# MLP block in four quarters: the up projection's product m2 by 512-column matmuls into four PSUM banks, in quarters 1 to 3

## Chip, cores and metric

One core of a Trainium2 chip runs the whole kernel in one launch. The metric is the device time of one execution in microseconds (us), the median of several runs. Engines are named as in the profile: PE is the TensorE matmul, PEld its weight load, DVE is VectorE, ACT is ScalarE, POOL is GpSimd, SP is SyncE.

## What is computed

The kernel is one decoder block: differential attention and causal pooling, merged by gates, and behind them an MLP. The change touches the MLP alone, the last half of the program. Cut to it, the reference reads:

```python
# SEQ = 512 rows, D_MODEL = 1024, D_FF = 4096, all float32
h2 = rmsnorm(x, norm_mlp_g[l])
z = jnp.square(jax.nn.relu(h2 @ w_up[l]))
x = x + (z @ w_down[l]).astype(x.dtype)
return rmsnorm(x, final_norm_g)
```

## The kernel before

**Quarters and products.** D_FF is cut into four quarters of 1024 columns. For quarter q the kernel runs `up(q)` and then `down(q)`, which adds the quarter's share of `z @ w_down` to `x1` in SBUF. Each of the two is a 2x2 block product done with seven block products in place of eight (a Strassen-type scheme). An operand block or a sum of blocks is called a form: A11, A12, A22 and S1 to S4. In quarters 1 to 3 the up projection's products are issued in this order: m1 (A11), m5 (S1), m6 (S2), m7 (S3), m4 (A22), m2 (A12, called the first block's second product), m3 (S4). m1, m6, m7 and m4 accumulate onto each other in the same banks, m5 and m3 in two others, m2 in its own.

**Precision.** Each float32 operand is cut into a high part that the PE takes (fp32r) and a low part that is the rest. A product is then high·high + high·low + low·high. For the weights ACT makes the high part (L112) and DVE the low part (L113). For z ACT makes the high part (L782) and DVE the low part (L785).

**Narrow and wide.** A product of the up projection has four units (i, p), of 128 d_ff rows each, with four weight blocks k. A narrow unit has 12 matmuls of 256 columns: for each k one of L821 (high weights by the high part of h2) and one of L824 (high weights by the low part), then four of L827 (low weights by the high part). Two units share one bank of 512 columns, so a narrow product takes two banks. A wide unit has 8: for each k one matmul of 512 columns (L818), whose moving operand is both parts of h2 side by side, then the four of L827 into the first half. Each wide unit fills a bank of its own, so the product takes four banks, and the two halves of a bank have yet to be added. In quarter 0 all products are narrow. In quarters 1 to 3 m1, m6, m7 and m4 are wide, and m5, m2 and m3 are narrow.

**Evictions.** `keep` copies a product out of PSUM into one of the float32 tiles `R` (rawz in the profile); for four banks it copies the second half with ACT (L850) and adds the first with DVE (L851). `join` adds a product to what lies in R already: by one add of 128x512 for each of two banks (L864), or, for four banks, by two adds of 128x256 for each bank (L860). `z_of` takes relu and square on ACT in halves of R (L873, L874). `sub` takes the differences of z blocks on DVE (L793, L796), and `zsplit` makes the two parts of a form of z. R[0] holds m1 + m2, and after `z_of` the form A11 of z (the tile z0); S1 of z is z4, A12 is z1, S2 is z5.

**Banks.** Two of the eight PSUM banks (2 and 3) are fixed, for the down projection's product m2 and what is summed on it; the other six are handed out in the order of a list, `acc.ids`. In names of the trace, um21_0 is the up projection's product m2, quarter 1, first bank; um11_0 to um11_3 are the four banks of m1, m6, m7 and m4; um51_0 and um51_1 those of m5 and m3; dm51 and dm11 are the down projection's first two products, S1 and A11, which take their banks from the same list.

**Down projection.** `down(q)` for q > 0 starts with S1, then A11, A12, S2, S4, S3, A22. `mms` issues, for each p, three matmuls: L932 (z high by weights high), L934 (z low by weights high), L935 (z high by weights low). `to_x1` adds finished banks to x1 on DVE (L952).

**What sets the order.** The program is written as a list of operations with their data. A scheduler turns it into one queue for each engine, and each engine works off its queue strictly in that order, waiting where a semaphore isn't there yet. An operation that is written down at one place can thus stand among operations of a later product. A few `after(...)` lines add an order by hand: among them, the weights' casts of quarter 3 for the up projection's A22 and S4 stand behind the joins that `state["joined", 0]` and `state["joined", 1]` name.

Of the kernel before, what the change touches and what calls it, by code (L numbers as in the profile page):

```python
# [51 lines left out]
def block_kernel(ctx, tc, xT, x_tok, gains, pos, consts, w_in, w_v, w_pool, w_out, w_up, w_dn, out):  # L52
# [4 lines left out]
    def after(later, earlier):  # L57
        tc.add_manual_dep(
            later.ins, earlier.ins.name,
            mybir.DependencyInfo(mybir.DependencyClass.NoSync, mybir.DependencyReason.DATA), reason="issue order",  # L60
        )

    state = {}
# [8 lines left out]
    def bank(i, name):  # L72
        return ps.tile([P, S], F32, tag=f"b{i}", name=name)
# [145 lines left out]
    for n in range(2):  # L219
        accs = [bank((0, 1, 2, 3, 4, 5, 6, 0)[4 * n + t], f"v{n}_{t}") for t in range(NT)]  # L220
        for kk in range(4):
# [24 lines left out]
            if n == 0 and 0 < kk < 3:  # L246
                i = kk - 1
# [94 lines left out]
    acc = Rot((0, 1, 2))  # L342
# [207 lines left out]
    A11, A12, A22, A21, S1, S2, S3, S4 = range(8)  # L550
# [18 lines left out]
    R = [rawz[:, i] for i in range(5)]  # L569
# [114 lines left out]
    acc = Rot((4, 5, 6, 7, 0, 1))  # L684
    m2 = [bank(2 + a, f"dm2_{a}") for a in range(2)]
# [84 lines left out]
    def halves(r):  # L770
        return [r[:, 2 * i : 2 * i + 2, :] for i in range(2)]
# [4 lines left out]
    def bank_view(pa):  # L776
        return [split_view(pa[i]) for i in range(2)]

    def zsplit(q, form, r):

        z = zform[form] = zf(f"z{form}_{q}")
        hi = zhi[q, form] = A.copy(out=z[:, 0], in_=r)  # L782
        if q == 0 and form == A11:
            after(hi, state[S4])
        lo = state["zlow", form] = V.tensor_tensor(out=z[:, 1], in0=r, in1=f(z[:, 0]), op=ALU.subtract)  # L785
        if q == 0 and form == A11:
            after(lo, state["join"])
# [10 lines left out]
    def up(q):  # L798
# [57 lines left out]
        def join(pa, r, hold=None):  # L856
            if len(pa) == 4:
                for i, ab in enumerate(map(split_view, pa)):
                    for j in range(2):
                        ins = V.tensor_tensor(out=r[:, i, :], in0=ab[:, j], in1=r[:, i, :], op=ALU.add)  # L860
                        state["joined", i] = ins
                return
            for a_, r_ in zip(bank_view(pa), halves(r)):
                state["join"] = V.tensor_tensor(out=r_, in0=a_, in1=r_, op=ALU.add)  # L864
                if hold:
                    after(state["join"], hold)

        def z_of(r, sign, pa=None):
            if pa and len(pa) == 4:
                keep(pa, r)  # L870
                pa = None
            for i, r_ in enumerate(halves(r)):
                A.activation(out=r_, in_=bank_view(pa)[i] if pa else r_, func=AF.Relu, scale=sign)  # L873
                ins = A.activation(out=r_, in_=r_, func=AF.Square)  # L874
            return ins

        wide = q > 0
        if wide:
            x, y, z = ((0, 1), (6, 7), (4, 5)) if q % 2 else ((4, 5), (6, 7), (0, 1))
            acc.ids, acc.n = x + y + z + x + y + x + z, 0  # L880
        ma = product(A11, "m1", wide=wide)
        keep(ma, R[0])
        if q == 0:
            forms_h2((S4,), slice(0, HS))

        def first_block():
            join(product(A12, "m2"), R[0], None if q else state[S2])
            z_of(R[0], 1.0)
            if q > 0:
                zsplit(q, A11, R[0])  # L890

        if q == 0:
            first_block()
# [3 lines left out]
        keep(ma, R[1])  # L897
        product(S3, "m7", onto=ma, wide=wide)
        join(ma, R[2])
        state["joined"] = state["join"]  # L900
        z_of(R[2], -1.0)
# [6 lines left out]
        if q > 0:  # L908
            first_block()
        product(S4, "m3", onto=mc)  # L910
        join(mc, R[1])
        z_of(R[1], -1.0)
        zsplit(q, A12, R[1])
# [118 lines left out]
    for q in range(4):  # L1032
        up(q)
        if q == 3:
            gfb, gmul = gain(big.tile([P, D], F32, tag="s4", name="gfb"), 1)
        down(q)
# [52 lines left out]
```

## Time and profile before

| | us |
|---|---|
| median of 3 runs | 669.75 |
| lowest and highest of them | 669.03, 670.06 |
| the profiled execution | 668.65 |
| its span, from first to last instruction | 666.8 |
| mean granted TensorE clock in it | 0.997 |

The times of single instructions all come from the profiled execution, whose own time is 668.65 us: 1.85 us more than its span, and 1.10 us less than the median. A row of a timeline reads: start in us from the span's start, duration in us, engine, line, operation, tile written <- tiles read, shape, how many follow each other (xcount), and in brackets the idle time before it with what ended it. A row of the windows gives the stretch, its length, and the busy us of each engine with the count of instructions in it.

In the timeline up(1) ends at 465.09 us, up(2) at 543.19 us and up(3) at 621.0 us, each with the last matmul of m3, and the first matmul of S1 in the down projection follows at once.

### The profile page before, as it was taken

How to read it: one execution, taken by the hardware profiler on the slowest of the kernel's cores; microseconds unless marked ns; L12 is line 12 of the kernel's file. 1: busy time of each engine (PE TensorE's matmuls, PEld its weight loads, DVE VectorE, ACT ScalarE, POOL GpSimd, SP SyncE). 2: the span in 40 equal slices, each digit the busy share in tenths (PEclk: the TensorE clock that was granted, in tenths of full speed). 3: DMA queues.
4: the chain of work that ended last, by engine and by line, in shares of the span. 5: the costliest groups of instructions: out<-in, count | busy, mean ns of one | idle time of the engine just before them, and what ended most of it. 6: DMA issues, size and time to landing. Idle time of an engine off the chain costs nothing.

```text
span 666.8 us, 9670 instructions
## 1 busy us (share of the span) xinstructions
PE 658.1 (99%) x3476; PEld 566.2 (85%) x3476; DVE 548.7 (82%) x958; ACT 470.3 (71%) x781; POOL 92.2 (14%) x115
## 2 busy tenths in 40 slices
PE   9999999999999999999999999999999999999995
PEld 7888888888888888888889988899889898899884
DVE  6855977799879987895688999777995889968996
ACT  8465587988878689976477975368563795456965
POOL 2001110031113011300202020202103021111020
PEclk9999999999999999999999999999999999999998
DMA  8416475355445466544886596786669676594863
GB/s 319 162 57 187 127 154 129 72 142 110 116 113 135 118 131 124 117 167 174 266 222 114 159 232 190 173 226 137 182 178 209 222 172 185 164 230 143 212 128 126
DMA packets 32736, 108.79 MB, mean 163 GB/s; under 512 B 4016, under 2 KB 4912, under 8 KB 32688
## 3 DMA queue, kind: packets, MB, share of 16 engines
q0 software_dynamic: 10512, 38.28, 32.1%
q1 hardware_dynamic: 21744, 69.38, 29.7%
q8 instruction: 27, 0.44, 0.3%
q10 hardware_dynamic: 432, 0.52, 0.2%
q14 instruction: 21, 0.17, 0.1%
HBM read 106.07 MB, written 2.10 MB: 162 GB/s over the span
## 4 chain that ended last, share of the span: by engine, by line
PE 98%; DMA 1%; ACT 0%; DVE 0%; SPq 0%; issue 0%
PE um L827 8%; PE dm L935 8%; PE dm L934 8%; PE dm L932 8%; PE um L818 7%; PE um L824 5%; PE um L821 5%; PE v L237 2%; PE o L430 2%; PE ga L137 2%; PE gp L133 2%; PE gp L137 2%; PE gp L134 2%; PE k L134 2%; PE ga L134 2%; PE k L133 2%
## 5 line engine op out<-in xcount | busy, mean ns | idle before, releaser
L934 PE MATMUL dm<-wh_dt,z 128*128 128x512 f32 (+1 forms) x128 | 49.4, 386 | 0.0
L935 PE MATMUL dm<-wl_dt,z 128*128 128x512 f32 (+1 forms) x128 | 49.0, 386 | 0.0
L112 ACT CAST wh_ut<-wga_uNone 128x1024 fp32r<-128x1024 f32 x24 | 25.1, 1054 | 33.7 <-DMA wga_uNone<-w_up 14.9
L932 PE MATMUL dm<-wh_dt,z 128*128 128x512 f32 (+1 forms) x128 | 48.6, 386 | 0.0
L952 DVE TENSOR_TENSOR x<-x,dm 128x512 f32<-128x512 f32 x48 | 32.4, 683 | 9.0 <-PE dm L935 8.8
L413 ACT ACTIVATE p<-p,st 128x128 f32<-128x128 f32 (+3 forms) x64 | 35.6, 557 | 5.8 <-DVE st L408 5.6
L782 ACT CAST z<-rawz 128x1024 fp32r<-128x1024 f32 x28 | 28.3, 1046 | 14.7 <-DVE rawz L793 13.0
L934 PE MATMUL dm<-wh_db,z 128*128 128x512 f32 x96 | 37.4, 391 | 0.0
L935 PE MATMUL dm<-wl_db,z 128*128 128x512 f32 x96 | 37.3, 390 | 0.0
L112 ACT CAST wh_ub<-wr_u 128x1024 fp32r<-128x1024 f32 x24 | 25.3, 1055 | 15.8 <-PE dm L934 5.3
L932 PE MATMUL dm<-wh_db,z 128*128 128x512 f32 x96 | 35.7, 389 | 0.0
L113 DVE TENSOR_TENSOR wl_ut<-wga_uNone,wh_ut 128x1024 fp32r<-128x1024 f32 x24 | 29.0, 1221 | 8.1 <-ACT wh_ut L112 8.0
L705 POOL DMA_DIRECT2D wga_dNone<-w_dn x16 | 13.8, 865 | 154.6 <-DVE wl_dt L113 154.4
L785 DVE TENSOR_TENSOR z<-rawz,z 128x1024 fp32r<-128x1024 f32 x28 | 33.3, 1219 | 1.5 <-ACT z L782 1.5
L112 ACT CAST wh_dt<-wga_dNone 128x1024 fp32r<-128x1024 f32 x24 | 24.8, 1045 | 11.5 <-DMA wga_dNone<-w_dn 6.4
L113 DVE TENSOR_TENSOR wl_ub<-wr_u,wh_ub 128x1024 fp32r<-128x1024 f32 x24 | 29.2, 1220 | 4.5 <-ACT wh_ub L112 4.5
L705 POOL DMA_DIRECT2D wga_uNone<-w_up x18 | 15.6, 864 | 111.2 <-DVE wl_ut L113 94.9
L827 PE MATMUL um<-gss,wl_ut 128*128 128x256 f32 x192 | 30.7, 282 | 0.0
L113 DVE TENSOR_TENSOR wl_dt<-wga_dNone,wh_dt 128x1024 fp32r<-128x1024 f32 x24 | 28.9, 1220 | 1.5 <-ACT wh_dt L112 1.5
L827 PEld LDWEIGHTS um<-gss,wl_ut 128*128 128x128 f32 x192 | 27.9, 190 | 2.0
L408 DVE CUSTOM_DVE_ANT_0 p<-s,mask 128x256 f32<-128x256 f32 (+3 forms) x52 | 27.2, 530 | 2.5 <-PE s L407 2.2
L934 PEld LDWEIGHTS dm<-wh_dt,z 128*128 128x128 f32 x128 | 24.0, 188 | 4.9
(335 smaller groups left out, 2191.6 us busy)
## 6 DMA issues: line engine op xcount, KB each, us to landing
wr_u<-w_up SPq DMA_DIRECT2D x24, 512.0 KB, 4.5
wr_d<-w_dn SPq DMA_DIRECT2D x24, 512.0 KB, 4.1
wga_uNone<-w_up POOLq DMA_DIRECT2D x18, 512.0 KB, 7.3
wga_dNone<-w_dn POOLq DMA_DIRECT2D x16, 512.0 KB, 6.8
wr_k<-w_in SPq DMA_DIRECT2D x8, 512.0 KB, 3.3
wr_ga<-w_in SPq DMA_DIRECT2D x8, 512.0 KB, 3.3
wr_gp<-w_in SPq DMA_DIRECT2D x8, 512.0 KB, 4.1
wl_ga<-w_in POOLq DMA_DIRECT2D x8, 512.0 KB, 6.3
```

The lines of the kernel that those rows point to most:

```text
L112: ins = A.copy(out=hi[:, sl], in_=raw[:, sl])
L113: state["low"] = (eng or G).tensor_tensor(out=lo[:, sl], in0=raw[:, sl], in1=f(hi)[:, sl], op=ALU.subtract)
L134: T.matmul(acc, lhsT=hi[:, c], rhs=rl[k], start=False, stop=False)
L413: A.activation(out=pr[:, c, :N], in_=pr[:, c, :N], func=AF.Exp, scale=-1.0, bias=st[:, c : c + 1], accum_out=st[:, 2 + c : 3 + c])
L785: lo = state["zlow", form] = V.tensor_tensor(out=z[:, 1], in0=r, in1=f(z[:, 0]), op=ALU.subtract)
L818: m = T.matmul(ab, lhsT=hi[:, c], rhs=both[:, k].rearrange("p a t -> p (a t)"), start=k == 0 and onto is None, stop=False, skip_group_chec ...
L821: m = T.matmul(a_, lhsT=hi[:, c], rhs=rh[:, k, :], start=p + k == 0 and onto is None, stop=False, skip_group_check=True)
L824: T.matmul(a_, lhsT=hi[:, c], rhs=rl[:, k, :], start=False, stop=False, skip_group_check=True)
L827: m = T.matmul(a_, lhsT=lo[:, c], rhs=rh[:, k, :], start=False, stop=k == 3, skip_group_check=True)
L932: m = T.matmul(a_, lhsT=zh, rhs=hi[:, sl], start=p == 0 and start, stop=False, skip_group_check=True)
L934: T.matmul(a_, lhsT=zl, rhs=hi[:, sl], start=False, stop=False, skip_group_check=True)
L935: end = T.matmul(a_, lhsT=zh, rhs=lo[:, sl], start=False, stop=p == 3, skip_group_check=True)
```

## The change

In quarters 1 to 3 m2 is wide as well. Its four banks need a place, so the three pairs of banks now rotate from quarter to quarter, and down's S1 takes m2's first pair and A11 its second. `join` of m2 takes the branch for four banks. Since `state["joined", i]` would now be overwritten by m2's join, it is set for R[2] alone (m7's join), as before.

```diff
                     for j in range(2):
                         ins = V.tensor_tensor(out=r[:, i, :], in0=ab[:, j], in1=r[:, i, :], op=ALU.add)
-                        state["joined", i] = ins
+                        if r is R[2]:
+                            state["joined", i] = ins
                 return
...
         wide = q > 0
         if wide:
-            x, y, z = ((0, 1), (6, 7), (4, 5)) if q % 2 else ((4, 5), (6, 7), (0, 1))
-            acc.ids, acc.n = x + y + z + x + y + x + z, 0
+            x, y, z = (((0, 1), (6, 7), (4, 5)), ((4, 5), (0, 1), (6, 7)), ((6, 7), (4, 5), (0, 1)))[q - 1]
+            acc.ids, acc.n = x + y + z + x + y + x + y + z, 0
         ma = product(A11, "m1", wide=wide)
...
         def first_block():
-            join(product(A12, "m2"), R[0], None if q else state[S2])
+            join(product(A12, "m2", wide=wide), R[0], None if q else state[S2])
             z_of(R[0], 1.0)
```

In counts: each of the three quarters has 32 matmuls of 512 and 256 columns for m2 (16 of L818, 16 of L827) where it had 48 of 256 columns, with as many weight loads; and 8 adds of 128x256 on DVE where it had 2 of 128x512. From line 861 on, lines of the changed kernel are numbered one higher: L864 is L865, L873 and L874 are L874 and L875, L932 to L935 are L933 to L936, L952 is L953.

The new instructions also stand at other places in the queues. First, PE at the end of up(1), where m2 is followed by m3's first bank (its second has been done by then) and that by down's S1. Before, all 24 matmuls of um21_0, all 24 of um21_1 and all 24 of um51_0 follow each other; the seam of the last two reads:

```order
L824 MATMUL um21_1_4408<-gab2_2979,wh_ub21_1_1_4403 128x256
L821 MATMUL um21_1_4408<-gab2_2979,wh_ub21_1_1_4403 128x256
L824 MATMUL um21_1_4408<-gab2_2979,wh_ub21_1_1_4403 128x256
L827 MATMUL um21_1_4408<-gab2_2979,wl_ub21_1_1_4404 128x256 x4
L821 MATMUL um51_0_4186<-gss3_2981,wh_ub22_1_0_4470 128x256
L824 MATMUL um51_0_4186<-gss3_2981,wh_ub22_1_0_4470 128x256
```

After, on the same engine at the same place:

```order
L827 MATMUL um21_1_4408<-gab2_2979,wl_ub21_1_0_4400 128x256 x4
L821 MATMUL um51_0_4186<-gss3_2981,wh_ub22_1_0_4462 128x256
L824 MATMUL um51_0_4186<-gss3_2981,wh_ub22_1_0_4462 128x256
L821 MATMUL um51_0_4186<-gss3_2981,wh_ub22_1_0_4462 128x256
L824 MATMUL um51_0_4186<-gss3_2981,wh_ub22_1_0_4462 128x256
L821 MATMUL um51_0_4186<-gss3_2981,wh_ub22_1_0_4462 128x256
L824 MATMUL um51_0_4186<-gss3_2981,wh_ub22_1_0_4462 128x256
L821 MATMUL um51_0_4186<-gss3_2981,wh_ub22_1_0_4462 128x256
L818 MATMUL um21_2_4409<-gab2_2979,wh_ub21_1_1_4403 128x512 x4
L827 MATMUL um21_2_4409<-gab2_2979,wl_ub21_1_1_4404 128x256 x4
```

m2's third bank now stands behind 7 matmuls of m3's first bank; its fourth stands 12 matmuls of m3 further on, and 5 of m3 follow it before down's S1.

Second, DVE at the same time, between the eviction of m4's third bank (um11_2) and that of m3's first bank (um51_0). Before:

```order
L851 TENSOR_TENSOR rawz_2982<-um11_2_4132,rawz_2982 128x256
L113 TENSOR_TENSOR wl_dt4_1_1_4567<-wga_dNone_1_1_4559,wh_dt4_1_1_4566 128x1024
L851 TENSOR_TENSOR rawz_2982<-um11_3_4133,rawz_2982 128x256
L864 TENSOR_TENSOR rawz_2982<-um21_0_4407,rawz_2982 128x512
L796 TENSOR_TENSOR rawz_2982<-rawz_2982 128x1024
L864 TENSOR_TENSOR rawz_2982<-um21_1_4408,rawz_2982 128x512
L785 TENSOR_TENSOR z4_1_4393<-rawz_2982,z4_1_4393 128x1024
L864 TENSOR_TENSOR rawz_2982<-um51_0_4186,rawz_2982 128x512
```

After:

```order
L851 TENSOR_TENSOR rawz_2982<-um11_2_4132,rawz_2982 128x256
L860 TENSOR_TENSOR rawz_2982<-um21_0_4407,rawz_2982 128x256
L113 TENSOR_TENSOR wl_dt4_1_1_4559<-wga_dNone_1_1_4551,wh_dt4_1_1_4558 128x1024
L860 TENSOR_TENSOR rawz_2982<-um21_0_4407,rawz_2982 128x256
L851 TENSOR_TENSOR rawz_2982<-um11_3_4133,rawz_2982 128x256
L860 TENSOR_TENSOR rawz_2982<-um21_1_4408,rawz_2982 128x256 x2
L860 TENSOR_TENSOR rawz_2982<-um21_2_4409,rawz_2982 128x256
L796 TENSOR_TENSOR rawz_2982<-rawz_2982 128x1024
L860 TENSOR_TENSOR rawz_2982<-um21_2_4409,rawz_2982 128x256
L860 TENSOR_TENSOR rawz_2982<-um21_3_4410,rawz_2982 128x256
L785 TENSOR_TENSOR z4_1_4393<-rawz_2982,z4_1_4393 128x1024
L860 TENSOR_TENSOR rawz_2982<-um21_3_4410,rawz_2982 128x256
```

One join now stands ahead of the weights' low part (L113), and the first join of the fourth bank stands ahead of the low part of z4 (L785). Behind these rows the queue of DVE is the same as before up to the low part of z1.

Third, ACT at the end of up(3) and the start of down(3), where z4, z0 and z1 are the forms S1, A11 and A12 of z, and wh_db11 and wh_db21 are weights of the down projection. Before:

```order
L782 CAST z4_3_5814<-rawz_2982 128x1024
L112 CAST wh_db11_3_0_6015<-wr_d0_3_0_5963 128x1024
L112 CAST wh_db11_3_1_6019<-wr_d0_3_1_5964 128x1024
L873 ACTIVATE rawz_2982<-rawz_2982 128x512
L874 ACTIVATE rawz_2982<-rawz_2982 128x512
L873 ACTIVATE rawz_2982<-rawz_2982 128x512
L782 CAST z0_3_5873<-rawz_2982 128x1024
L112 CAST wh_db21_3_0_6054<-wr21_d3_6051 128x1024
```

After:

```order
L782 CAST z4_3_5798<-rawz_2982 128x1024
L112 CAST wh_db11_3_0_5991<-wr_d0_3_0_5939 128x1024
L112 CAST wh_db11_3_1_5995<-wr_d0_3_1_5940 128x1024
L874 ACTIVATE rawz_2982<-rawz_2982 128x512 x2
L875 ACTIVATE rawz_2982<-rawz_2982 128x512 x2
L874 ACTIVATE rawz_2982<-rawz_2982 128x512
L782 CAST z0_3_5849<-rawz_2982 128x1024
L112 CAST wh_db21_3_0_6030<-wr21_d3_6027 128x1024
```

Ahead of the high part of z0 there are now three relus and two squares where there were two relus and one square. The last of these relus is that of the second half of m3's block, which needs DVE's join of um53_1.

On DVE, the queue of quarter 3 after z4's low part was: low part of wh_db11's first half, join of um53_0, low part of the second half, join of um53_1, z0's low part. The two joins of um23_3 now stand among these, and the x1 addition of dm53_0 stands ahead of z0's low part. In quarter 2 the low part of z1 now stands ahead of both low parts of wh_db21, and the low part of z5 behind both low parts of wh_dt5 (the weights of the down projection's S2), an x1 addition and an L793.

## Prediction

> **What bounds the kernel now.** I read the page first (share of busy time, then the chain that ended last), then the waits of PE, then the stretches around the change, then single rows.
>
> ```profile
> span 666.8 us, 9670 instructions
> PE 658.1 (99%) x3476; PEld 566.2 (85%) x3476; DVE 548.7 (82%) x958; ACT 470.3 (71%) x781; POOL 92.2 (14%) x115
> PE 98%; DMA 1%; ACT 0%; DVE 0%; SPq 0%; issue 0%
> ```
>
> PE is busy 99% of the span, and the chain runs on it for 98%. The view of PE's waits from 340 us to the end has no row. So any PE time that goes is gained, if PE finds its operands, and any new PE wait is lost. The average hides that DVE has room in one stage and none in the next:
>
> ```profile
> core 0: us, PE busy (x) PEld busy (x) DVE busy (x) ACT busy (x) POOL busy (x), PEclk, DMA share, GB/s
> 456.00:465.10 9.10, 9.10 (x78) 9.10 (x77) 6.45 (x8) 6.71 (x11) 3.51 (x4) 1.00 0.75 132
> 465.10:476.50 11.40, 11.40 (x53) 9.28 (x51) 11.19 (x12) 10.86 (x14) 0.00 (x0) 1.00 0.77 211
> 543.20:554.60 11.40, 11.40 (x53) 9.28 (x51) 11.22 (x13) 10.97 (x14) 0.00 (x0) 1.00 0.81 220
> 621.00:632.40 11.40, 11.40 (x53) 9.43 (x52) 11.40 (x13) 11.30 (x15) 0.00 (x0) 1.00 0.87 234
> ```
>
> The first row is the end of up(1), where m2 and half of m3 run; the other three are the first two products of down(1), down(2) and down(3). In these DVE is busy 11.19, 11.22 and 11.40 of 11.40 us. Work that slides over that border out of up(q) delays everything on DVE behind it, and PE reads its results there.
>
> **PE's saving.**
>
> ```profile
> 453.65 1.09 PE L818 MATMUL um<-gab,wh_ut 128*128 128x512 f32 x4
> 454.58 0.63 PE L827 MATMUL um<-gab,wl_ut 128*128 128x256 f32 x4
> 455.05 1.09 PE L818 MATMUL um<-gab,wh_ut 128*128 128x512 f32 x4
> 456.45 0.28 PE L821 MATMUL um<-gab,wh_ub 128*128 128x256 f32 x1
> 457.89 0.28 PE L821 MATMUL um<-gab,wh_ub 128*128 128x256 f32 x1
> ```
>
> A wide unit of m4 starts at 453.65 and the next at 455.05: 1.40 us. A narrow unit of m2 goes from 456.45 to 457.89: 1.44 us, twelve steps of 0.12. Four units a quarter give 4 x 0.04 = 0.16 us, and three quarters **0.48 us**. The PE ends m3 0.16 us earlier.
>
> The Trainium skill (TensorE: Matmul & The Clock Gate, Back-to-back issue gap) gives an isolated warm matmul N/2.4 + 2.5 ns, by which two of 256 columns in place of one of 512 cost 2.5 ns more: estimated from that page, 48 x 2.5 ns = 0.12 us, and the time would be 0.36 us above mine. The rows decide for 0.48.
>
> **DVE's price.**
>
> ```profile
> L860 DVE TENSOR_TENSOR rawz<-um,rawz 128x256 f32<-128x256 f32 x24 | 9.3, 417 | 0.1
> L864 DVE TENSOR_TENSOR rawz<-um,rawz 128x512 f32<-128x512 f32 x18 | 12.3, 686 | 1.6 <-PE um L827 1.6
> 450.17 0.75 DVE L860 TENSOR_TENSOR rawz<-um,rawz 128x256 f32<-128x256 f32 x2
> ```
>
> Eight adds of 417 ns replace two of 686: 1.96 us more busy time a quarter. Instructions overlap by some 0.085 us (two in a row take 0.75, so a step of 0.33; likewise 0.60 for 512 columns and 1.135 for 1024), so in steps the price is 8 x 0.33 - 2 x 0.60 = 1.45 us. The question is how much of it idle time takes in. Quarter 1 before:
>
> ```profile
> 457.77 1.23 DVE L113 TENSOR_TENSOR wl_dt<-wga_dNone,wh_dt 128x1024 fp32r<-128x1024 f32 x1 [0.63 <-ACT wh_dt L112]
> 458.91 0.42 DVE L851 TENSOR_TENSOR rawz<-um,rawz 128x256 f32<-128x256 f32 x1
> 459.53 0.69 DVE L864 TENSOR_TENSOR rawz<-um,rawz 128x512 f32<-128x512 f32 x1 [0.20 <-PE um L827]
> 461.44 1.23 DVE L796 TENSOR_TENSOR rawz<-rawz 128x1024 f32<-128x1024 f32 x1 [1.22 <-ACT rawz L874]
> 463.79 1.23 DVE L785 TENSOR_TENSOR z<-rawz,z 128x1024 fp32r<-128x1024 f32 x1 [0.52 <-ACT z L782]
> 465.29 0.69 DVE L864 TENSOR_TENSOR rawz<-um,rawz 128x512 f32<-128x512 f32 x1 [0.28 <-PE um L827]
> 475.15 2.35 DVE L785 TENSOR_TENSOR z<-rawz,z 128x1024 fp32r<-128x1024 f32 x2
> 465.09 0.63 PE L932 MATMUL dm<-wh_dt,z 128*128 128x512 f32 x2
> 465.56 0.39 PE L934 MATMUL dm<-wh_dt,z 128*128 128x512 f32 x1
> 476.45 0.47 PE L934 MATMUL dm<-wh_db,z 128*128 128x512 f32 x1
> ```
>
> The brackets add up to 0.63 + 0.20 + 1.22 + 0.52 + 0.28 = 2.85 us of idle time, twice the price; what counts is where it lies. Two lags: down's first matmul follows m3 at 465.09, and DVE starts m3's join at 465.29, 0.20 us behind PE. z1's low part ends at 475.15 + 1.22 = 476.37, and PE's L934, which takes 0.39 elsewhere, took 0.47 at 476.45, so its work began at about 476.53, 0.16 us behind DVE.
>
> **Quarter 1.** In the new order PE ends um21_0 at 456.45 + 1.40 = 457.85, um21_2 after 7 matmuls of m3 at 461.49, um21_3 after 12 more at 464.33, m3 at 464.93. On DVE the first join stands ahead of L113 and starts at 457.85 + 0.20 = 458.05; from there, in steps, L113 at 458.38, a join at 459.52, L851 at 459.85, two joins to 460.84. um21_2's join waits for PE to 461.69, and L796 follows at 462.02 (before: 461.44). um21_2's second join follows, then um21_3's first waits for PE till 464.53. Queued behind that wait is z4's low part: 464.86 to 466.09, where it ended at 465.02. PE wants it for L934 at 465.56 - 0.16 = 465.40 and gets it at 466.25: **0.85 us of new wait**. Behind it DVE runs um21_3's second join and reaches um51_0's at 466.33, where it was at 465.29. From there to z1's low part DVE was full before (11.19 of 11.40 us), so that part ends 1.0 us later. PE was already waiting for it a little (the 0.47), so all of the 1.0 comes through: 0.85 - 0.16 at z4, the rest at z1. Quarter 1: **+1.0**, between 0 (idle time takes all in) and 1.3 (all 1.45 comes through, less 0.16).
>
> **Quarter 2.**
>
> ```profile
> 543.39 0.69 DVE L864 TENSOR_TENSOR rawz<-um,rawz 128x512 f32<-128x512 f32 x1 [0.16 <-PE um L827]
> 546.97 1.22 DVE L785 TENSOR_TENSOR z<-rawz,z 128x1024 fp32r<-128x1024 f32 x1
> 554.55 0.47 PE L934 MATMUL dm<-wh_db,z 128*128 128x512 f32 x1
> 559.85 0.39 PE L934 MATMUL dm<-wh_dt,z 128*128 128x512 f32 x1
> ```
>
> L796 stands ahead of um22_2's and um22_3's joins, so z4's low part isn't late. Two joins (0.66) lie between it and z0's low part, of which idle time takes 0.16 to 0.25: z0 starts near 547.4. z1's low part is moved forward, so the short wait at 554.55 (0.08) goes. From z0's on, nine operations of 1024 columns (z0, z1, two of L793, one of L796, four of L113) and two additions now stand ahead of z5's low part: 547.4 + 9 x 1.135 + 2 x 0.60 = 558.8, and it ends at 560.0. PE wants it for L934 at 559.85, less 0.24, plus up to 0.45 as two matmuls of wh_db22 move ahead of it: 559.6 to 560.1, against 560.2 with the lag. A wait of 0.1 to 0.6, less 0.24: -0.1 to +0.4, and with the lateness of wh_db22's low parts up to +0.7. I take **+0.2**.
>
> **Quarter 3.**
>
> ```profile
> 622.83 0.69 DVE L864 TENSOR_TENSOR rawz<-um,rawz 128x512 f32<-128x512 f32 x1
> 623.43 1.22 DVE L785 TENSOR_TENSOR z<-rawz,z 128x1024 fp32r<-128x1024 f32 x1
> 630.31 2.35 DVE L785 TENSOR_TENSOR z<-rawz,z 128x1024 fp32r<-128x1024 f32 x2
> 622.36 1.04 ACT L782 CAST z<-rawz 128x1024 fp32r<-128x1024 f32 x1
> 626.95 0.39 PE L934 MATMUL dm<-wh_db,z 128*128 128x512 f32 x1
> 632.39 0.39 PE L934 MATMUL dm<-wh_db,z 128*128 128x512 f32 x1
> 645.85 0.50 PE L935 MATMUL dm<-wl_db,z 128*128 128x512 f32 x1
> ```
>
> um53_1's join ended at 622.83 + 0.69 = 623.52; two joins of um23_3 now stand before it: 624.2. On ACT z0's high part waited for no such join (622.36 to 623.40); now the relu that needs um53_1 stands ahead: it ends at about 624.8, the cast at 625.8, z0's low part at 627.1. PE wants that at 626.95 - 0.16 = 626.79 and gets it at 627.23: 0.44 us. Behind it DVE runs L793, an addition, two of L113 and L796 without a gap (625.85 + 5 x 1.135 + 0.60 = 632.1): z1's low part ends at 633.35, and PE, wanting it at 632.39 - 0.16 + 0.44 = 632.67, gets it at 633.51: 0.84. The row at 645.85 (0.50 in place of 0.39) shows that wl_db22, made by ACT behind z1's cast and then by a DMA, comes just in time: ACT's delay there may add 0 to 0.4, and I take 0.1. 0.44 + 0.84 + 0.10 - 0.16: **+1.2**.
>
> **Edits at nothing.** The rotation of banks: down's S1 takes um21_0's and um21_1's banks, whose last join ends at 460.9, and PE needs it at 464.9; A11 takes um21_2's and um21_3's, free at 466.4, needed 24 matmuls of 0.23 after 464.9, at 470.4. If that cover of 4 us went, PE would wait for the join. SP's queue is in the same order; on POOL one weight DMA of quarter 3 changes places with its neighbour, for which I count nothing, since PE has no wait there. `state["joined"]` names the same joins as before.
>
> **Sum.** 1.0 + 0.2 + 1.2 = +2.4 us, in which the 0.48 of PE is counted already: the profiled execution of 668.65 (span 666.8) would be 671.05, and the median, 1.10 above it, **672.15**. I forecast 672.2.
>
> **Rivals.**
> - **The joins are hidden (669.3).** In each quarter there is more idle time on DVE (2.85 us in quarter 1) than the joins cost (1.45), and only PE's 0.48 remains: 669.75 - 0.48. It decides at z4's low part: if it ends by 465.24, 0.16 ahead of PE's need at 465.40, nothing follows in quarter 1 but the full DVE; the ACT chain of quarter 3 would have to make up 0.4 as well. Against it stand 11.40 busy of 11.40 us. The Trainium skill (Perfetto Trace Analysis, Identifying the Most-Contended Engine) says that the engine with the highest occupancy is to be optimized first, here PE with its weight loads at 85% against DVE's 82%; by that the saving would count in full, and the stretches above, which it also tells one to look at apart, speak against it.
> - **Nothing is taken in (673.6).** All 1.45 come through in each quarter, as DVE reaches the border that much later and is full behind it: 3 x 1.45 - 0.48 = +3.9. It decides by whether um51_0's join in quarter 1 starts 1.0 or 1.45 us later; in quarter 2, z1's part ahead of its old place speaks against it.
> - **Weight loads bound (664).** In the first window PEld is busy 9.10 of 9.10 us, and 48 loads go; at a step of 0.12 each that is 5.8 us. Against it: the wide unit has 4 loads fewer and is only 0.04 us shorter.
> - That the change doesn't do what it says can be left out: the queues show the wide matmuls and the eight joins.
>
> **How the numbers follow.** About 0.2% (1.34 us) is what a measurement of this kernel tells from no change, so "same" is 668.41 to 671.09. Forecast 0.72, spread over the open ends of quarters 1 (0 to 1.0), 2 (-0.1 to 0.7) and 3 (0.7 to 1.6): 670.3 to 673.1. Hidden 0.16, nothing taken in 0.09, loads 0.03. The range 669.9 to 674.0 leaves out the hidden case and loads, most of 0.2. Same: 0.14 of the hidden case and 0.06 of the forecast's low end, 0.20; faster 0.05 (loads and 0.02 of the hidden case); slower 0.75.
>
> **What would show it.** Right: units of m2 at 1.40 us; DVE's L785 of z4 in quarter 1 behind a wait for um21_3, ending near 466.1; PE's waits on DVE's L785 at z4 and z1 of quarter 1 and z0 and z1 of quarter 3, some 0.4 to 0.9 us each, and nearly none in quarter 2. Wrong: no such waits (hidden), waits of like size in quarter 2 too (nothing taken in), a stretch of up(q) shorter by 1 us or more (loads).

## The result, and the profile after

| | before | changed |
|---|---|---|
| median of 6 runs, us | 669.90 | 674.35 |
| lowest and highest | 669.03, 670.33 | 672.63, 675.79 |
| profiled execution, us (span) | 668.65 (666.8) | 673.09 (671.3) |

The changed kernel is slower: 1.0067 of before, 95% interval 1.0056 to 1.0077. The forecast was 672.2, in a range of 669.9 to 674.0: the sign was right, the size was about half of what was measured (+2.4 against +4.45 us), and the measured time lies 0.35 us above the range.

The profiled execution of the changed kernel, its page and the view of PE's waits from 430 us on:

```profile
span 671.3 us, 9598 instructions
PE 660.4 (98%) x3428; PEld 563.5 (84%) x3428; DVE 552.5 (82%) x976; ACT 470.2 (70%) x781; POOL 92.0 (14%) x115
engine line waited for: us in total, times, longest us
PE dm L935 <- DVE z L785: 2.4, 5, 0.6
```

Before, that view of waits had no row. Now PE waits five times by this view, each time in a down projection, in front of the matmul that reads the low part of a form of z.

Where the time lies is read best by quarters. In the table a quarter runs from the first matmul of m5 in `up(q)` to that of the next quarter, and quarter 3 from there to PE's last matmul; the values are differences of starts in PE's timeline, in us.

| kernel | quarter 1 | quarter 2 | quarter 3 |
|---|---|---|---|
| before | 77.87 | 78.08 | 72.41 |
| changed | 78.81 | 79.56 | 74.38 |
| difference (forecast) | +0.94 (+1.0) | +1.48 (+0.2) | +1.97 (+1.2) |

Quarter 1 came as forecast; quarters 2 and 3 did not. Quarter 1, timeline of DVE and PE of the changed kernel:

```profile
456.53 1.09 PE L818 MATMUL um<-gab,wh_ub 128*128 128x512 f32 x4
457.94 1.09 PE L818 MATMUL um<-gab,wh_ub 128*128 128x512 f32 x4
458.13 0.42 DVE L860 TENSOR_TENSOR rawz<-um,rawz 128x256 f32<-128x256 f32 x1 [0.81 <-PE um L827]
461.78 0.42 DVE L860 TENSOR_TENSOR rawz<-um,rawz 128x256 f32<-128x256 f32 x1 [0.64 <-PE um L827]
464.61 0.42 DVE L860 TENSOR_TENSOR rawz<-um,rawz 128x256 f32<-128x256 f32 x1 [0.94 <-PE um L827]
464.95 1.22 DVE L785 TENSOR_TENSOR z<-rawz,z 128x1024 fp32r<-128x1024 f32 x1
466.42 0.68 DVE L865 TENSOR_TENSOR rawz<-um,rawz 128x512 f32<-128x512 f32 x1
466.23 0.50 PE L935 MATMUL dm<-wh_dt,z 128*128 128x512 f32 x1 [0.59 <-DVE z L785]
477.43 0.50 PE L935 MATMUL dm<-wh_db,z 128*128 128x512 f32 x1
```

A unit of m2 takes 1.41 us. DVE waits 0.94 us for m2's fourth bank with z4's low part queued behind, and that part ends at 466.17 (forecast 466.09). PE's L935 starts at 466.23 (forecast 466.25). Quarters 2 and 3, from the timelines of DVE, ACT and PE, first three rows of the kernel before and then the changed one:

```profile
533.23 1.22 DVE L743 TENSOR_TENSOR wga_dNone<-wr_d,wal_d 128x1024 f32<-128x1024 f32 x1
542.00 1.23 DVE L785 TENSOR_TENSOR z<-rawz,z 128x1024 fp32r<-128x1024 f32 x1 [0.52 <-ACT z L782]
610.96 1.22 DVE L743 TENSOR_TENSOR wga_dNone<-wr_d,wal_d 128x1024 f32<-128x1024 f32 x1 [1.69 <-DMA wr_d<-w_dn]
```

```profile
535.72 1.23 DVE L743 TENSOR_TENSOR wga_dNone<-wr_d,wal_d 128x1024 f32<-128x1024 f32 x1 [2.00 <-DMA wr_d<-w_dn]
543.91 1.23 DVE L785 TENSOR_TENSOR z<-rawz,z 128x1024 fp32r<-128x1024 f32 x1 [0.32 <-ACT z L782]
545.19 0.50 PE L935 MATMUL dm<-wh_dt,z 128*128 128x512 f32 x1 [0.46 <-DVE z L785]
547.57 0.63 ACT L874 ACTIVATE rawz<-rawz 128x512 f32<-128x512 f32 x1 [0.17 <-DVE rawz L860]
548.90 2.00 ACT L782 CAST z<-rawz 128x1024 fp32r<-128x1024 f32 x2
551.26 0.50 PE L935 MATMUL dm<-wh_db,z 128*128 128x512 f32 x1 [0.29 <-DVE z L785]
614.23 1.23 DVE L743 TENSOR_TENSOR wga_dNone<-wr_d,wal_d 128x1024 f32<-128x1024 f32 x1 [1.69 <-DMA wr_d<-w_dn]
626.77 0.68 DVE L865 TENSOR_TENSOR rawz<-um,rawz 128x512 f32<-128x512 f32 x1
627.53 0.62 ACT L874 ACTIVATE rawz<-rawz 128x512 f32<-128x512 f32 x1
628.05 1.03 ACT L782 CAST z<-rawz 128x1024 fp32r<-128x1024 f32 x1
629.12 1.23 DVE L785 TENSOR_TENSOR z<-rawz,z 128x1024 fp32r<-128x1024 f32 x1 [1.07 <-ACT z L782]
629.14 0.73 PE L933 MATMUL dm<-wh_db,z 128*128 128x512 f32 x2
630.40 0.50 PE L935 MATMUL dm<-wh_db,z 128*128 128x512 f32 x1 [0.53 <-DVE z L785]
636.67 0.50 PE L935 MATMUL dm<-wh_db,z 128*128 128x512 f32 x1 [0.54 <-DVE z L785]
```

In quarter 2 PE waits for z4 (545.19), which the prediction excluded, and for z0 (551.26), which it put at nothing. Behind the first stands a weight tile: DVE idles 2.00 us in front of L743, which needs down's last tile of first weights; before, it did not idle there. Behind the second stands ACT: a relu waits for DVE's last join of m2 (547.57), and z0's high part follows square after relu at 548.90. In quarter 3 DVE itself idles 1.07 us in front of z0's low part, waiting for ACT's cast; PE waits for the high part (629.14), for the low part (630.40), and for z1 (636.67). The weights of z4 are late here as well: L743 starts 24.75 us into quarter 3, and 23.98 us before.

### The profile page after: what moved, and what is told of

It is laid out like the page before. It is cut to its first block, busy times and chain, and to the rows that moved or that the text cites. A ratio compares the mean times of both kernels' runs of the same rounds, so it can differ in the third digit from the quotient of the medians.

```text
span 671.3 us, 9598 instructions
## 1 busy us (share of the span) xinstructions
PE 660.4 (98%) x3428; PEld 563.5 (84%) x3428; DVE 552.5 (82%) x976; ACT 470.2 (70%) x781; POOL 92.0 (14%) x115
## 4 chain that ended last, share of the span: by engine, by line
PE 51%; issue 26%; DMA 17%; DVE 4%; ACT 2%; POOL 0%; SPq 0%; POOLq 0%; ACTq 0%; DVEq 0%
DMA wga_uNone<-w_up 11%; DMA wga_dNone<-w_dn 5%; PE v L237 2%; PE o L430 2%; PE ga L137 2%; PE gp L133 2%; PE gp L134 2%; PE gp L137 2%; PE k L134 2%; PE ga L134 2%; PE k L133 2%; PE k L137 2%; PE ga L133 2%; PE v L239 2%; PE v L238 2%
## 5 line engine op out<-in xcount | busy, mean ns | idle before, releaser
L935 PE MATMUL dm<-wh_dt,z 128*128 128x512 f32 (+1 forms) x128 | 49.8, 389 | 1.1 <-DVE z L785 1.1
L936 PE MATMUL dm<-wl_dt,z 128*128 128x512 f32 (+1 forms) x128 | 49.0, 386 | 0.0
L933 PE MATMUL dm<-wh_dt,z 128*128 128x512 f32 (+1 forms) x128 | 48.8, 387 | 0.0
L953 DVE TENSOR_TENSOR x<-x,dm 128x512 f32<-128x512 f32 x48 | 32.0, 679 | 9.5 <-PE dm L936 9.3
L935 PE MATMUL dm<-wh_db,z 128*128 128x512 f32 x96 | 37.5, 394 | 1.4 <-DVE z L785 1.4
L936 PE MATMUL dm<-wl_db,z 128*128 128x512 f32 x96 | 37.1, 390 | 0.0
L113 DVE TENSOR_TENSOR wl_ut<-wga_uNone,wh_ut 128x1024 fp32r<-128x1024 f32 x24 | 29.0, 1220 | 9.7 <-ACT wh_ut L112 9.5
L785 DVE TENSOR_TENSOR z<-rawz,z 128x1024 fp32r<-128x1024 f32 x28 | 33.5, 1218 | 3.0 <-ACT z L782 3.0
L933 PE MATMUL dm<-wh_db,z 128*128 128x512 f32 x96 | 35.9, 391 | 0.1
L113 DVE TENSOR_TENSOR wl_ub<-wr_u,wh_ub 128x1024 fp32r<-128x1024 f32 x24 | 29.1, 1218 | 4.8 <-ACT wh_ub L112 4.7
L112 ACT CAST wh_dt<-wga_dNone 128x1024 fp32r<-128x1024 f32 x24 | 24.5, 1046 | 9.0 <-DMA wga_dNone<-w_dn 3.2
L827 PE MATMUL um<-gss,wl_ut 128*128 128x256 f32 x192 | 30.7, 282 | 0.0
L935 PEld LDWEIGHTS dm<-wh_dt,z 128*128 128x128 f32 x128 | 24.0, 188 | 7.0 <-DVE z L785 2.4
L827 PEld LDWEIGHTS um<-gss,wl_ut 128*128 128x128 f32 x192 | 27.9, 190 | 2.0
L113 DVE TENSOR_TENSOR wl_dt<-wga_dNone,wh_dt 128x1024 fp32r<-128x1024 f32 x24 | 28.6, 1216 | 0.7 <-ACT wh_dt L112 0.7
```

The costliest lines, as they stand in the source:

```text
L112: ins = A.copy(out=hi[:, sl], in_=raw[:, sl])
L113: state["low"] = (eng or G).tensor_tensor(out=lo[:, sl], in0=raw[:, sl], in1=f(hi)[:, sl], op=ALU.subtract)
L827: m = T.matmul(a_, lhsT=lo[:, c], rhs=rh[:, k, :], start=False, stop=k == 3, skip_group_check=True)
L933: m = T.matmul(a_, lhsT=zh, rhs=hi[:, sl], start=p == 0 and start, stop=False, skip_group_check=True)
L935: T.matmul(a_, lhsT=zl, rhs=hi[:, sl], start=False, stop=False, skip_group_check=True)
L936: end = T.matmul(a_, lhsT=zh, rhs=lo[:, sl], start=False, stop=p == 3, skip_group_check=True)
```

## Experiments

Two theories stood first. **Carried**: quarters 2 and 3 were sized right but come in late from the quarter before. **Local**: each pays its own price. Then, for the mechanism, **amount** (DVE does eight instructions for two) against **order** (m2's banks are finished late, and their joins fall among the low parts). Ratios are to runs of the kernel before on the same chip.

**m2 wide in one quarter alone** (`only_q1`, `only_q2`, `only_q3`).

```diff
-            join(product(A12, "m2", wide=wide), R[0], None if q else state[S2])
+            join(product(A12, "m2", wide=q == 1), R[0], None if q else state[S2])
```

(2 or 3 in place of 1; the banks rotate only in that quarter.)

> m2 is wide in quarter 1 alone. In the profile of the changed kernel quarter 1 cost PE +0.98 us net, quarter 2 +1.45, quarter 3 +1.95, against +1.0, +0.2 and +1.2 in the prediction. Theory 'carried': quarter 1 was sized right, and quarters 2 and 3 cost more than worked out because DVE and the weight loads come into them already late from the quarter before. It expects +1.0 us here at the end of quarter 1, of which quarters 2 and 3 keep all: about 670.9 (before 669.9). Theory 'local': each quarter pays only its own price, wherever the others stand: also 670.9. If the loss is made good later (slack behind quarter 1), 669.9.

> m2 is wide in quarter 2 alone. 'Carried': without quarter 1's lateness the price is that of the prediction, +0.2 (up to +0.7): 670.1 to 670.6. 'Local': +1.45 as in the changed kernel's profile: 671.3.

> m2 is wide in quarter 3 alone. 'Carried': the prediction's price of +1.2: 671.1, with the last join of m3 (um53_1) ending about 0.7 us after its place before. 'Local': +1.95: 671.9, with that join about 1.4 us later than before.

Measured, in this order: 671.51 (1.0026, 1.0016 to 1.0036), 671.16 (1.0018, 1.0006 to 1.0029) and 671.62 us (1.0034, 1.0023 to 1.0045), with before at 669.52. The quarter concerned took 78.77, 79.67 and 74.26 us. Quarters 2 and 3 cost as much alone as they do together, and the three ratios add up to 1.0078, not below the 1.0067 of the whole change, so "carried" falls as it was worded: the prices do not shrink to those of the prediction. That they are local is not shown. `only_q1` costs 1.7 us (1.0026), more than the +1.0 of both theories, and its quarter 2, which is the kernel before's, took 78.73 us; in four profiles whose first two quarters are both the kernel before's it took 78.08 to 78.43. So a little of quarter 1's change seems to reach quarter 2. And the waits are not the same ones. With quarter 2 alone z4 comes in time, and PE waits in up(2), in front of m4, instead; the like times of 79.67 and 79.56 us are made of different waits. With quarter 3 alone the weights of z4 come in time (L743 starts 23.74 us into the quarter), PE hardly waits for z0 (a step of 0.31 us in front of the row at 627.88, where 0.23 is the rule), and its longest wait is for wl_db22. Here are the row of quarter 2 alone and three of quarter 3 alone:

```profile
527.03 1.20 PE L818 MATMUL um<-gab,wh_ut 128*128 128x512 f32 x4 [0.47 <-DVE rawz L860]
```

```profile
611.72 1.22 DVE L743 TENSOR_TENSOR wga_dNone<-wr_d,wal_d 128x1024 f32<-128x1024 f32 x1 [1.47 <-DMA wr_d<-w_dn]
627.88 0.50 PE L938 MATMUL dm<-wh_db,z 128*128 128x512 f32 x1
648.46 0.50 PE L939 MATMUL dm<-wl_db,z 128*128 128x512 f32 x1 [0.64 <-DMA wl_db<-w_dn]
```

ACT prepares the tile wl_db22 and a DMA completes it: ACT's last step of it (L722) ended 15.81 us behind the first matmul of down(3), 14.66 before, and the tile landed at 26.5 us, 24.8 before. In the changed kernel it landed at 26.6 us; PE does not wait for it there because it has already lost 2.0 us in front of z0 and z1. In profiles whose quarter 3 is unchanged this wait was also 0 to 0.6 us, so part of it comes and goes.

**m3's first bank behind m2** (`m2_first`).

```diff
             elif form == S4:
                 after(first[-1], state["m4"])
+                if q:
+                    after(first[-1], state["m2"])
+            elif form == A12 and q:
+                state["m2"] = m
```

> As the changed kernel in all three quarters, but m3's first bank may not start on PE before m2's last matmul, so that the four banks of m2 are finished one behind the other and joined while PE runs m3. Same instructions, other order. Theory 'order' (the price comes from the late third and fourth bank of m2, whose joins fall among the low parts of z and of the weights): in quarter 1 the fourth bank is done on PE near 462.1 instead of 464.3 and z4's low part ends near 465.4, so that only PE's saving is left: about 669.5 to 670.0. Theory 'amount' (DVE has eight adds in place of two and no room for the 1.45 us a quarter, wherever they stand): 673 to 674.4.

Measured: 670.50 us, 1.0013 (1.0003 to 1.0024). The same instructions in another order cost 0.9 us in place of 4.5. Quarter 1 took 78.13 us, quarter 2 79.03, quarter 3 72.28. DVE and PE in quarter 1:

```profile
461.41 1.09 DVE L864 TENSOR_TENSOR rawz<-um,rawz 128x256 f32<-128x256 f32 x3 [0.25 <-PE um L827]
463.54 0.88 DVE L864 TENSOR_TENSOR rawz<-um,rawz 128x256 f32<-128x256 f32 x2
464.75 1.23 DVE L785 TENSOR_TENSOR z<-rawz,z 128x1024 fp32r<-128x1024 f32 x1 [0.33 <-ACT z L782]
466.03 0.50 PE L939 MATMUL dm<-wh_dt,z 128*128 128x512 f32 x1
```

All joins are done by 464.42, 1.07 us before PE starts down's S1 at 465.49 in this profile, and z4's low part waits for ACT alone. That is for "order", but not all of it: quarter 2 keeps 0.95 us, and the time lies 0.5 us above the top of what "order" expected.

**Half of the joins left out (`half_join`); eight DVE instructions on narrow banks (`eight`).** The first keeps the order and takes the amount away, the second does the reverse. The result of `half_join` lacks the left-out product, and that of `eight` is another because of the maxima.

```diff
-                    for j in range(2):
+                    for j in range(2 if r is R[2] else 1):
```

```diff
+                if q and r is R[0]:
+                    for j in range(2):
+                        state["join"] = V.tensor_tensor(out=r_[:, j], in0=a_[:, j], in1=r_[:, j], op=ALU.add)
+                        V.tensor_tensor(out=r_[:, j], in0=r_[:, j], in1=a_[:, j], op=ALU.max)
+                    continue
```

> As the changed kernel, but m2's second half of each bank (its product with the low part of h2) is left out of the join: four adds of 128x256 a quarter in place of eight, 1.32 us of steps where the kernel before has 1.20. PE is as in the changed kernel. Theory 'amount' (DVE's extra time is the price, wherever it stands): nearly no extra time is left, 669.5 to 669.9. Theory 'order' (the price comes from joins that wait for m2's late fourth bank, in front of z's low part): that join still stands ahead of z4's low part and waits until 464.5, so each quarter keeps about 0.7 us: 671 to 672, with a PE wait of 0.7 to 0.9 us in front of L935 at the start of the down projection in quarter 1.

> The kernel before (m2 narrow, in two banks), but DVE does eight instructions of 128x256 for m2's join in each quarter: four adds, and four maxima of the result with the same bank that are no part of the computation. DVE's load is that of the changed kernel without its late banks. 'Amount': 3 x 1.45 us come through as in the changed kernel, and PE saves nothing: 674 to 675. 'Order': m2's banks are done before m3, so the eight fall into DVE's idle time: 669.9 to 671.

Half the joins: 671.20 us, 1.0029 (1.0018 to 1.0040), quarters at 78.46, 79.43 and 73.42. PE at the start of down(1):

```profile
466.08 0.50 PE L935 MATMUL dm<-wh_dt,z 128*128 128x512 f32 x1 [0.47 <-DVE z L785]
```

The step from the matmul before (465.22) is 0.86 us where 0.23 is the rule: with DVE's load almost that of before, the wait behind m2's late bank stays. Eight on narrow banks: 670.31 us, 1.0016 (1.0006 to 1.0026), and the same matmul follows without a wait:

```profile
465.89 0.39 PE L939 MATMUL dm<-wh_dt,z 128*128 128x512 f32 x1
```

Its quarters 1 and 2 took 77.85 and 78.14 us, as before: the eight instructions themselves are hidden there. Quarter 3 took 73.73, with one long wait for wl_db22 (a step of 1.20 us). Both speak for "order", and against "amount" as the whole cause. Behind the late banks the amount does count: with four joins there in place of eight the price is 1.9 us and not 4.5.

**The late joins behind z4, the last relu behind z0** (`places`).

```diff
+                        elif i == 3:
+                            after(ins, state["zlow", S1])
...
+                if q and i and r is R[1]:
+                    after(ins, zhi[q, A11])
```

> The changed kernel with two orders added: the joins of m2's fourth bank stand behind z4's low part on DVE (this moves them in quarter 1; they were there in quarters 2 and 3), and the last relu of m3's block behind z0's high part on ACT (quarter 3). Theory 'full DVE' (what is moved away from z4 comes back at z1, since DVE works without a gap from there to z1's low part): quarter 1 stays within 0.2 us of the changed kernel's 78.8 us (from down's first weights of m5 in one quarter to those in the next, 77.9 before), with the wait at z4 nearly gone and that at z1 longer by as much; in all 673.5 to 674.3. Theory 'each wait by itself': the wait of 0.75 at z4 goes and nothing takes its place, 78.1 us, and 673.0 or less in all.

Measured: 673.15 us, 1.0059 (1.0046 to 1.0072); quarters at 78.50, 79.14 and 73.21. The start of down(1) and of its A12:

```profile
466.49 0.39 PE L939 MATMUL dm<-wh_dt,z 128*128 128x512 f32 x1
478.40 0.50 PE L939 MATMUL dm<-wh_db,z 128*128 128x512 f32 x1 [0.57 <-DVE z L785]
```

The wait for z4 is gone, and the step in front of z1's low part has grown from 0.42 us to 1.02. Of 0.76 us taken away at z4 0.6 came back at z1: in quarter 1 "full DVE" is nearly right (78.50, 0.3 below the changed kernel, where 0.2 was allowed). In quarter 3 PE no longer waits for z0, and the quarter takes 1.17 us less. But this does not show that the relu was the cause: the weights of z4 came earlier in this profile as well (L743 starts 23.66 us into the quarter, in the changed kernel 24.75), and with quarter 3 alone, where the relu does stand in z0's way, PE hardly waited for z0 either. (The work behind PE's last matmul took 8.40 us in this profile and 7.46 in the others, so not all of this reaches the time.)

**The rotation of banks alone** (`rotate`).

```diff
+            acc.ids, acc.n = x + y + z + x + x + y + z, 0
```

> The kernel before with the new rotation of banks alone: m2 is narrow in the first pair, down's S1 takes that same pair, A11 the second, and the pairs rotate. If the banks cost nothing, as predicted: 669.9 within 0.3. If the rotation makes a first matmul wait for a join, 670.5 or more, with a PE wait in front of down's S1 or A11, or of the next quarter's m1.

Measured: 669.56 against 669.27 us, 1.0011 (1.0001 to 1.0020), with quarters 1 and 2 at 77.85 and 77.91 and no wait of PE in front of S1, A11 or m1. So no bank makes PE wait. Quarter 3 took 73.00 us, 0.6 more than before, with a PE wait for wl_db22; whether the rotation has a part in that is not shown.

**Two profiles more.**

> The kernel before once more, for a second profile. In kernels whose quarter 2 is the kernel before's, the second weight tile of down(2) landed 25.3 us (m2 wide in quarter 1 alone) after down's first weights of m5 were due, in the first profile of before 23.5 us. If that landing and the one of wl_db22 in quarter 3 differ from execution to execution whatever the kernel, quarter 2 comes out between 78.0 and 78.8 us here, and quarter 3 between 72.2 and 73.0. If the wide m2 makes them late, 78.1 and 72.4 as in the first profile.

> The changed kernel once more, for a second profile. Price fixed by the order of instructions: quarter 1 at 78.8 us as before within 0.1. Quarter 2 (79.56) and quarter 3 (74.38) may move by the landings of weights: 79.0 to 79.8 and 74.2 to 75.2. In all 673 to 676.

Before: quarters 77.87, 78.19 and 72.25, and the tile landed at 23.56 us after the first matmul of m5, as at first (23.49). Changed: 78.77, 79.77 and 75.11, the tile at 25.94 (25.70 at first). So quarter 1 is fixed within 0.04 us, the late tile belongs to the kernel, and quarter 3 moves by 0.7.

**ACT's work for the final gain behind wl_db22**, in the kernel before (`gfb_late`) and in m2_first (`first_gfb`).

```diff
-                    A.mul(out=lo, in_=f(hi), mul=-1.0)
+                    ins = A.mul(out=lo, in_=f(hi), mul=-1.0)
+                    if c:
+                        after(gmul, ins)
```

> The kernel before, with one ACT instruction of 1.05 us (the final gain's factor, L574) held behind the two that make the low weights wl_db22 of quarter 3, for which PE waits 0.1 us in the first profile and 0.6 to 1.1 us in the profiles of three experiments. If ACT's place in that chain is what PE waits for: the wait goes, 669.3 becomes 668.5 to 669.1. If the DMA that completes wl_db22 is held by its queue and not by ACT: no change, 669.3.

> m2 wide in three quarters with m3's first bank behind it (m2_first, 1.0013 of before), and the gain's factor held behind wl_db22 as well. If order is all that stood against the change, this is where it would beat the kernel before: 668.8 to 669.5. If the rest of m2_first's loss is in quarter 2 (z4's wait), 669.8 to 670.4.

Measured: 670.36 (1.0003, 0.9992 to 1.0015) and 670.30 us (1.0009, 0.9997 to 1.0021). Neither beats the kernel before. In the first, ACT was done with wl_db22 0.4 to 0.7 us earlier in its quarter than in the two profiles of before, and PE still waited some 0.5 us: the tile landed 24.5 us behind the first matmul of down(3), as in those two profiles (24.8 and 24.5). It is the DMA that holds it.

**What makes the tile of quarter 2 late.** The DMA view of the transfer, from issue to landing, in the changed kernel and before (queue, kind: packets, MB, share; then the issue with its us to landing):

```profile
q1 hardware_dynamic: 207, 0.72, 41.0%
q8 instruction: 1, 0.02, 1.6%
q14 instruction: 1, 0.01, 0.7%
wr_d<-w_dn SPq DMA_DIRECT2D x1, 512.0 KB, 5.3
```

```profile
q1 hardware_dynamic: 207, 0.72, 62.1%
wr_d<-w_dn SPq DMA_DIRECT2D x1, 512.0 KB, 3.2
```

The data are the same; after the change packets of instructions fall into the transfer. All seven profiles so far of kernels that are wide in quarter 1 have a packet of 16 KB (queue q8) there, and the tile took 4.65 to 5.42 us. The seven that are not have none of 16 KB there, and six of them took 3.19 to 3.50 us, `eight` among them with a packet of 8 KB (q14) inside; `only_q2` took 4.37 with no packet inside. In these seven the 16 KB packet falls some 3 us earlier, into the transfer of the tile before, and that one took 3.76 to 4.26 us, where it took 3.04 to 3.38 in the other seven. Three kernels move the packet by 32 PE instructions in quarter 0 (`less16`, `more16`, `first_more16`; one execution each):

```diff
-                        T.matmul(a_, lhsT=hi[:, c], rhs=rl[:, k, :], start=False, stop=False, skip_group_check=True)
+                        if q or form != A12:
+                            T.matmul(a_, lhsT=hi[:, c], rhs=rl[:, k, :], start=False, stop=False, skip_group_check=True)
```

(in the kernel before; in the other two `for _ in range(1 if q or form != A12 else 2):` stands there.)

> The kernel before, but quarter 0's m2 leaves out the 16 matmuls by the low part of h2 (part of the computation), so that PE has 32 instructions fewer (16 matmuls and 16 weight loads), as many as the wide m2 saves in quarter 1. Theory 'fetch': the 16 KB packets of instructions for PE then fall about 3 us later, as in the kernels that are wide in quarter 1: 22 to 23 us after down's... after the start of m5 in quarter 2 in place of 19, into the transfer of the last weight tile, which then takes 4.6 to 5.4 us in place of 3.2 to 3.5, and quarter 2 comes out at 78.4 to 78.9. Theory 'other traffic' (the late tile comes from the wide m2's timing of other loads): 3.2 to 3.5 us, and 78.0 to 78.4. The time in all is about 2 us below before, since 16 matmuls of 0.12 us are gone.

> The changed kernel, but quarter 0's m2 does the 16 matmuls by the low part of h2 twice (so its result is another), which puts the 32 instructions back on PE. 'Fetch': the packet falls 19 us after the start of m5 in quarter 2 again, the last weight tile takes 3.2 to 3.5 us, and the wait of 0.63 to 0.69 us for z4's low part in quarter 2 shrinks to below 0.1, so that quarter 2 takes 78.8 to 79.0 in place of 79.56 and 79.77. 'Other traffic': 5.3 us, and 79.5 to 79.8. In all 1.9 us more in quarter 0.

> m2_first with the same 32 instructions put back in quarter 0. 'Fetch': quarter 2 at 78.0 to 78.4 in place of 79.03, with no PE wait in front of m2's fourth bank and below 0.1 us at z4. 'Other traffic': 78.9 to 79.1.

In the kernel before, with 32 instructions fewer and m2 narrow everywhere, the packet is in the transfer and PE waits at z4:

```profile
q8 instruction: 1, 0.02, 1.5%
wr_d<-w_dn SPq DMA_DIRECT2D x1, 512.0 KB, 5.4
543.83 0.50 PE L935 MATMUL dm<-wh_dt,z 128*128 128x512 f32 x1 [0.48 <-DVE z L785]
```

Its quarter 2 took 79.42 us, 1.34 more than before, even above the expected 78.4 to 78.9; about 0.75 of that is lost in front of z4. In all it took 668.95 us, 0.56 below before's 669.51 and not 2, as quarter 2 takes most of the gain back. In the changed kernel with 32 instructions more (675.16 us) the 16 KB packet is back at 18.96 us, ahead of the last tile. The tile's transfer took 4.2 us (expected 3.2 to 3.5) with an 8 KB packet inside, there is no wait at z4, and quarter 2 took 78.87 us as expected, 0.7 to 0.9 below the two profiles without them. So "fetch" holds for the changed kernel. In m2_first with 32 instructions more (672.66 us) the packet moved too, to 19.67 us, but little was gained by it: the tile before took 5.28 us and the last one 4.42, PE still waits for z4 (0.4 us), and quarter 2 took 79.57, not 78.0 to 78.4. Another wait stands in up(2) there:

```profile
542.19 1.20 PE L818 MATMUL um<-gab,wh_ub 128*128 128x512 f32 x4 [0.58 <-DVE rawz L856]
```

m2's fourth bank is the bank that m4's fourth unit used. With m2 in four banks PE needs both of m4's last evictions, which stand on DVE behind the low parts of down's weights (L113).

## Why the prediction was right in sign and short in size

**What bounds the kernel, PE's saving: right.** PE bounds it; units of m2 take 1.41 us (forecast 1.40), and up(1) and up(3) are 0.17 and 0.13 us shorter (34.06 to 33.89, 34.05 to 33.92; forecast 0.16). By the formula of the Trainium skill (TensorE: Matmul & The Clock Gate, Back-to-back issue gap) it would have been an estimated 0.04 a quarter; the measurement decides for the rows. The rotation of banks makes no matmul wait, as forecast.

**Quarter 1: right, step by step.** The join that waits for m2's fourth bank, z4's low part at 466.17 for 466.09, m3's join at 466.42 for 466.33, the rest at z1: +0.94 for +1.0. m3's join comes 1.05 us later in its quarter, the forecast's 1.0 and not the 1.45 of the rival "nothing is taken in". The `places` run bears out that z1 would have taken back most of what z4 gave.

**"DVE's price" of 1.45 us a quarter, as an amount: misleading.** Eight narrow adds cost nothing in quarters 1 and 2 when they come early (77.85 and 78.14), and four late ones keep 0.6 us of quarter 1's 0.94. The rival "nothing is taken in" (673.6) came nearest in time, and its sign, waits of like size in quarter 2, did come; but `less16` and `more16` tie the longest of them to a late tile and not to the amount of adds, so its nearness is luck.

**Quarter 2, the first failed step**: "z4's low part isn't late". It ended 1.04 us behind the first matmul of down(2), 0.04 before. The order on DVE was read rightly; the tile in front of it landed 2.2 us later in its quarter. `less16` shows this without a wide m2, `more16` shows the changed kernel without it: about 0.7 to 0.9 of quarter 2's 1.5 us. The prediction priced the 48 matmuls taken from PE, but not that fewer instructions move the packets of instructions. The wait for z5, which it did name, came at 0.17 us, inside its 0.1 to 0.6.

**Quarter 2, the second**: "z0 starts near 547.4", counted along DVE's queue alone. z0's low part needs ACT's cast, that a square and a relu, and the relu m2's last join, which stands behind a weight's low part: it started at 549.98, near 549.0 without the 1.0 us by which the quarter began later. PE's step in front of it was 0.68 us instead of 0.23. This wait does not hang on the late tile: it is as long in `more16` and `only_q2` (steps of 0.71), where z4 is in time.

**Quarter 3, the third: z0's term was too small, 0.44 for 1.2 us.** um53_1's join was put at 624.2 and came at 627.46, or 624.96 without the 2.50 us of the quarters before, and ACT's relu and cast and z0's low part followed it as forecast. The prediction let the weights of z4 arrive as before; they came 0.8 us later in their quarter (L743). In the four profiles with this quarter 3 (`only_q3`, the changed kernel, `more16`, the changed kernel's second) L743 starts 23.74, 24.75, 25.07 and 25.30 us into the quarter, and PE loses 0.2, 1.2, 1.5 and 1.5 us at z0, the slower steps behind the waits included. So z0's term is one of late weights more than of the relu in its way; what makes these weights late stays open. z1's term was right: 0.8 for 0.84. wl_db22, put at 0.1 of 0 to 0.4, was mis-sized as well: it lands 1.8 us later, which is hidden behind the other waits in the changed kernel, and costs 0.9 in the kernel that is wide in quarter 3 alone (a step of 1.02 and a slower one behind it). How quarter 3 divides differs from profile to profile (74.38, 75.11, and 74.26 alone).

**What a wait costs.** Behind each wait the next step is 0.33 to 0.34 us instead of 0.23, so a wait costs 0.1 more than it lasts (466.23 to 466.56, the L936 behind it). Where the prediction had a wait, its lag of 0.16 covers this without naming it: PE starts 0.06 us behind z4's low part (466.17, 466.23), and the slower step makes up the other 0.1. Where it had none, this is missing too. Before, the last three quarters had two such steps, after the change nine: 7 x 0.1, some 0.7 us of the difference.

No version beat the kernel before. The best with a wide m2 lies at 1.0009 to 1.0013 of it: the 0.48 us that the change can win is smaller than what it risks.

## What to carry to other kernels

Price a change by when each result is complete and by every engine on the way to its reader, not by busy time: the same instructions cost 4.5 us with m2's banks late and some 0.9 us with them early. If a product takes more banks, ask whose evictions now stand before it, and whether the scheduler will put another product's matmuls between its banks. Where a saving is 0.5 us in 670, waits of tenths in loads and casts decide the sign; look for those with no slack in the profile before.

## What the runs showed of the hardware

The time of a load goes with where packets of instructions fall. The page of both kernels has this row:

```profile
q8 instruction: 27, 0.44, 0.3%
```

27 packets of 16 KB come over the span, one in some 25 us, and one of them inside a 512 KB load goes with 5.3 us in place of 3.2. Taking 32 instructions from PE moved it by 3.5 us (from 18.96 to 22.49 us after the start of m5 in less16), which points to q8 carrying PE's. The Trainium skill (Perfetto Trace Analysis, The 4-stage abstract model) says that an instruction has 64 bytes. By that figure, as an estimate, 256 are in a packet and 6912 in 27, and the trace comes within 1% of it, with 3476 matmuls and 3476 weight loads before. The rate in 40 slices of 0.2 us from 529 us on shows how the tile is late in the changed kernel: its bulk is through at 533.0, and single packets follow until it lands at 535.6.

```profile
GB/s 143 246 123 225 430 410 328 328 369 21 0 205 82 123 246 307 389 410 328 369 82 41 20 0 20 0 41 20 20 20 20 0 0 0 0 0 0 0 0 0
```

Which of the 16 DMA engines these packets wait for, the view does not show.
